# Later due times for queued splits in a two-block transformer kernel with float32 weights

## The chip, the core and the metric

The kernel runs on one core of one Trainium2 chip. The metric is the device time of one execution in microseconds (us). Five engines work side by side, each through its own queue in order: TensorE (PE, matrix products), VectorE (DVE), ScalarE (ACT), GpSimd (POOL) and SyncE (SP, which issues most transfers). Sixteen DMA engines move the data.

## The reference

The input `x` has 256 positions of 1024 channels. Two blocks follow one another, each of two layers. A layer is a feed-forward stage, a mixer and a second feed-forward stage, each added to `x`; the first block ends with a normalisation.

```python
x = x + 0.5 * swiglu(rms_norm(x, ffn1_norm[l]), ffn1_w_in[l], ffn1_w_out[l])   # 1024 -> 2 x 2816 -> 1024
x = x + mixer(rms_norm(x, mix_norm[l]), mix_w_in[l], ...)
x = x + 0.5 * swiglu(rms_norm(x, ffn2_norm[l]), ffn2_w_in[l], ffn2_w_out[l])
```

The mixer of the first block projects to q, k, v (8 heads of 64), to a Fourier branch and to two gates. Its attention adds a table of relative positions and a mask of columns to the scores. The mixer of the second block has three other kinds of attention; the change doesn't touch it. All weights are float32 and stay in the chip's main memory until they are used once.

## The kernel before, in words

**Products.** Every projection goes through `dense`. It takes weights in units of four 128-row tiles (1 MB, one transfer into one of four `raw` buffers, line 118) and splits each pair of tiles into a high and a low part, `whi` (a cast on ACT, line 341) and `wlo` (a subtraction on DVE, line 342). The activations are split in the same way (`xhi`, `xlo`, `hhi`, `hlo`). A product is then three matrix products (lines 145 to 147), so a pair of weight tiles feeds 2 tiles x 2 halves of the positions x 3 = 12 of them. `whi` and `wlo` have two buffers each, and two more while a feed-forward stage or the first mixer runs.

**Feed-forward stage (`ffn`).** Six steps compute gate and up product, 512 columns each (the last 256), with `h` = silu(gate) x up. `h` has to be transposed for the second product. Steps are grouped (`GROUPS`): steps 0 and 1 make eight 128-column tiles, steps 2 and 3 eight, step 4 four, step 5 two. For each group `queue_t` queues the transpose: `turned` transposes 32x32 blocks on DVE (`hB`, line 94), and two transfers issued by POOL carry it out to main memory and back in another order (`hop`, then `hT`, lines 96 and 97). Then `hT` is split into `hhi` and `hlo`, in pieces of up to four tiles and one half of the positions: four splits for a group of eight, two for the smaller ones. The second product is over all 22 tiles, once for each half `n` of the columns; it was written as 16 tiles, a `drain`, and 6 tiles. After `n` = 0, `queue_x` queues the same kind of transpose for the first half of the new `x`, with four parts.

**The queue.** `later(fn, ticks)` puts a function into a list with a due time; `advance` raises the tick by one and runs the first function that is due, one a tick; `drain` runs all that is left. `unit` calls `advance` after each split of a pair of weight tiles, so a tick is one such split:

```python
ins = self.split(hi[:, :m, :off], lo[:, :m, :off], raw[:, j : j + m, :off])
with self.tc.issue_after(ins.ins):
    if not self.hold:
        self.advance()
```

`split` returns its subtraction. `issue_after` orders what is written inside the block behind that instruction, if it is on the same engine. Apart from such constraints the source's order isn't the order of an engine's queue: the framework's scheduler works through the program with times of its own, and an instruction enters its engine's queue when, by these times, its inputs are there and its buffer is free.

**First mixer (`mixer1`).** Four steps of 512 columns (q, k, v, Fourier). q and k are transposed by `turned` into `qT` and `kT`, and split into `qh`, `kq`, `kzh` after all four steps, when the queue has been drained. `bias1` loads the table of a pair of heads by four transfers of 96 KB (`rawb`, line 437, issued by ACT) into one of the four `raw` buffers, and adds the column mask on DVE (`bias`, line 439, three buffers). Pairs 0 and 1 are loaded ahead of the first step, pairs 2 and 3 in the attention's loop. After the attention and the Fourier branch come four steps for the gates and the output products.

Of the kernel before, what the change touches and what calls it, by code (L numbers as in the profile page):

```python
# [18 lines left out]
P = 128  # L19
T = 2  # L20
# [6 lines left out]
class Net:  # L27
# [47 lines left out]

    def queue_t(self, h, nk, hhi, hlo, k0):
        hv = self.turned(lambda t: h[t], nk, self.b("hT", n=2048))
        lag = 7 if nk > 2 else 6
        step = min(nk, 4)
        for i in range(0, nk, step):  # L80
            for t in range(T):
                o = lambda d: d[:, k0 + i : k0 + i + step, t * P : (t + 1) * P].rearrange(
                    "p k (q j) -> p k q j", j=32)
                self.later(lambda hi=o(hhi), lo=o(hlo), s=hv[:, i : i + step, t]: self.split(hi, lo, s), lag)
# [116 lines left out]
    def queue_x(self, li):  # L201
        hv = self.turned(lambda t: self.x[:, t, :512], 4, self.xtile())

        def part(k):
            g = self.gcol[:, li, k : k + 1] if isinstance(li, int) else li[:, k : k + 1]
            for t in range(T):
                o = lambda d: d[:, k, t * P : (t + 1) * P].rearrange("p (q j) -> p q j", j=32)
                self.split(o(self.xhi), o(self.xlo), hv[:, k, t], scale=g)

        for k in range(4):  # L210
            self.later(lambda k=k: part(k), 7)

    def xt_half(self, n, li):
        nc = self.nc
# [29 lines left out]
    def ffn(self, w_in, w_out, nxt):  # L244
        nc = self.nc
        rs = None
        self.open()
        self.xtile = lambda: self.b("hT", n=2048)
        self.more(2)
        hhi = self.big.tile([P, 22, T * P], F32R, name=self.nm("hhi"), tag="hhi")  # L250
        hlo = self.big.tile([P, 22, T * P], F32R, name=self.nm("hlo"), tag="hlo")
        self.hold = True
        for c in range(6):
            if c < 5:
                pg = self.dense(self.xhi, self.xlo, KD, [(w_in, c * 512, 512)])
                pu = self.dense(self.xhi, self.xlo, KD, [(w_in, DFF + c * 512, 512)])
                w = 512
                gs, us = pg, pu
            else:
                pp = self.dense(self.xhi, self.xlo, KD, [(w_in, 2560, 256), (w_in, DFF + 2560, 256)])  # L260
                w = 256
                gs, us = pp, [q[:, 256:512] for q in pp]
            if rs is None:
                rs = self.rstd()
            if c == 0:
                self.hold = False
                self.drain()
            if c in GROUPS:
                h, c0 = [self.b("h", n=1024, bufs=4) for _ in range(T)], c
            for t in range(T):  # L270
                sl = self.b("sl", bufs=3)
                nc.scalar.activation(sl[:, :w], gs[t][:, :w], AF.Silu, scale=rs[:, t : t + 1])  # L272
                o = (c - c0) * 512
                nc.vector.scalar_tensor_tensor(h[t][:, o : o + w], us[t][:, :w], rs[:, t : t + 1], sl[:, :w],  # L274
                                               op0=ALU.mult, op1=ALU.mult)
            if c == 5 or c + 1 in GROUPS:
                self.queue_t(h, (o + w) // P, hhi, hlo, c0 * 4)
        for n in range(2):
            ps = self.dense(hhi, hlo, 16, [(w_out, n * 512, 512)], last=False)
            self.drain()  # L280
            self.dense(hhi, hlo, 6, [(w_out, n * 512, 512)], ps=ps, k0=16, first=False)
            for t in range(T):
                xs = self.x[:, t, n * 512 : (n + 1) * 512]
                nc.vector.scalar_tensor_tensor(xs, ps[t], 0.5, xs, op0=ALU.mult, op1=ALU.add)
            self.after(n, nxt)
        self.xtile = None
        self.more(0)
        self.close()
# [120 lines left out]
class Mix1:  # L409
# [18 lines left out]
    def bias1(self, l, p):  # L428
        nc = self.nc
        rp = self.a["rpbp"]  # L430
        bt = self.raw.tile([P, 4, 512], F32, name=self.nm("rawb"), tag="raw").rearrange("p a b -> p (a b)")[:, :768]
        bv = bt.rearrange("p (h e k) -> p h e k", h=2, e=6)
        for half in range(2):
            for h in range(2):
                src = bass.AP(tensor=rp.tensor, offset=((l * 8 + 2 * p + h) * 15 + 5 - half) * 127,
                              ap=[[1, 64], [127, 6], [1, 64]])
                nc.scalar.dma_start(out=bv[half * 64 : half * 64 + 64, h], in_=src)
        bias = self.big.tile([P, 768], F32, name=self.nm("bias"), tag="bias", bufs=3)
        nc.vector.tensor_tensor(bias.rearrange("p (h k) -> p h k", k=64)[:, :, ::-1],
                                bt.rearrange("p (h k) -> p h k", k=64),  # L440
                                self.cmask.unsqueeze(1).broadcast_to([P, 12, 64]), op=ALU.add)
        return bias

    def mixer1(self, l, nxt):
        nc, a, tc = self.nc, self.a, self.tc
# [6 lines left out]
        kzh = big.tile([P, 4, 2, 256], F32R, name=self.nm("kzh"), tag="mlo")  # L452
        kq = big.tile([P, 4096], F32R, name=self.nm("kq"), tag="m1th")
        kzl = kq[:, :2048].rearrange("p (k i t) -> p k i t", k=4, i=2)
        ql = kq[:, 2048:3072].rearrange("p (k t) -> p k t", k=4)
        qT = big.tile([P, 1024], F32, name=self.nm("qT"), tag="m1fhi")
        kT = big.tile([P, 1024], F32, name=self.nm("kT"), tag="m1flo")
        qh, vn = tl("qh", [P, 4, 256], F32R), tl("vn", [P, T, 512])
        u = big.tile([P, KD, 256], F32R, name=self.nm("u"), tag="mhi").rearrange("p (h t a) b -> p h t (a b)", h=2, t=2)
        uhi, ulo = u[:, 0], u[:, 1]  # L460
        bt = [self.bias1(l, p) for p in range(2)]
        self.zpad(kzh.bitcast(F32))
        self.zpad(kzl.bitcast(F32))
        rs = rq = None
        for c in range(4):
            ps = self.dense(self.xhi, self.xlo, KD, [(w_in, c * 512, 512)])
            if c == 0:
                rs = self.rstd()
                rq = self.sm.tile([P, T], F32, name=self.nm("rq"), tag="rq")
                nc.vector.tensor_single_scalar(rq, rs, 0.125, op=ALU.mult)  # L470
            if c < 2:
                h = []
                for t in range(T):
                    ht = self.b("h", bufs=4)
                    sc = (rq if c == 0 else rs)[:, t : t + 1]
                    if t == 0:
                        nc.scalar.activation(ht, ps[t], AF.Copy, scale=sc)
                    else:
                        nc.vector.tensor_scalar(out=ht, in0=ps[t], scalar1=sc, scalar2=None, op0=ALU.mult)
                    h.append(ht)  # L480
                turned = self.turned(lambda t, h=h: h[t], 4, qT if c == 0 else kT)
                qv, kv = (turned, None) if c == 0 else (qv, turned)
            elif c == 2:
                for t in range(T):
                    sc = rs[:, t : t + 1]
                    if t == 0:
                        nc.scalar.activation(vn[:, t], ps[t], AF.Copy, scale=sc)
                    else:
                        nc.vector.tensor_scalar(out=vn[:, t], in0=ps[t], scalar1=sc, scalar2=None, op0=ALU.mult)
            else:  # L490
                for t in range(T):
                    sc = rs[:, t : t + 1]
                    nc.scalar.activation(uhi[:, t], ps[t], AF.Copy, scale=sc)
                    nc.vector.scalar_tensor_tensor(ulo[:, t], ps[t], sc, uhi[:, t].bitcast(F32),
                                                   op0=ALU.mult, op1=ALU.subtract)
        self.drain()
        for t in range(T):
            o = lambda d: d[:, :, t * P : (t + 1) * P].rearrange("p k (q j) -> p k q j", j=32)
            self.split(o(qh), o(ql), qv[:, :, t])
            for i in range(2):  # L500
                r = slice(64 * i, 64 * i + 64)
                self.split(o(kzh[:, :, i])[r], o(kzl[:, :, i])[r], kv[r, :, t])
        ohi, olo = tl("ohi", [P, 4, 256], F32R), tl("olo", [P, 4, 256], F32R)
        for p in range(4):
            if p % 2 == 0:
# [8 lines left out]
                nc.vector.tensor_tensor(ona[:, t, (p % 2) * P : (p % 2 + 1) * P].rearrange("p (j d) -> p j d", j=2),  # L514
                                        po, rc.unsqueeze(2).broadcast_to([P, 2, 64]), op=ALU.mult)
            if p < 2:
                bt.append(self.bias1(l, p + 2))
            if p % 2 == 1:
                self.tr4(lambda j, t: ona[:, t, j * P : (j + 1) * P],
                         ohi[:, p - 1 : p + 1, :].rearrange("p a b -> p (a b)"),  # L520
# [22 lines left out]
        for c in range(4):  # L543
            ps = self.dense(self.xhi, self.xlo, KD, [(w_in, 2048 + c * 512, 512)])
# [3 lines left out]
            for t in range(T):  # L548
                d = th[:, t, c * 512 : (c + 1) * 512]
# [618 lines left out]
```

## Time and profile before

| | |
|---|---|
| time before, median of 3 runs | 2280.21 us (2274.0 to 2283.1) |
| profiled execution, its own time | 2291.64 us |
| its span, first to last instruction | 2289.8 us |
| PE busy | 99% of the span, 10446 products |
| PE weight loads (PEld) busy | 81% |
| DVE, ACT, POOL busy | 68%, 50%, 3% |
| DMA engines | 203 GB/s on average |
| mean granted clock of PE | 0.996 |

Engines' times overlap, so the shares don't add up. A product counts as busy until its result is written while the next one has begun, so a busy PE isn't one at its peak; but where PE is idle, it has nothing to do. The granted clock is a share of 2.4 GHz; it has two levels, and a mean between them over a stretch says how long each lasted.

### The profile page before, as it was taken

How to read it: one execution, taken by the hardware profiler on the slowest of the kernel's cores; microseconds unless marked ns; L12 is line 12 of the kernel's file. 1: busy time of each engine (PE TensorE's matmuls, PEld its weight loads, DVE VectorE, ACT ScalarE, POOL GpSimd, SP SyncE). 2: the span in 40 equal slices, each digit the busy share in tenths (PEclk: the TensorE clock that was granted, in tenths of full speed). 3: DMA queues.
4: the chain of work that ended last, by engine and by line, in shares of the span. 5: the costliest groups of instructions: out<-in, count | busy, mean ns of one | idle time of the engine just before them, and what ended most of it. 6: DMA issues, size and time to landing. Idle time of an engine off the chain costs nothing.

```text
span 2289.8 us, 27621 instructions
## 1 busy us (share of the span) xinstructions
PE 2260.2 (99%) x10446; PEld 1861.1 (81%) x10446; DVE 1547.2 (68%) x2549; ACT 1148.8 (50%) x1674; POOL 78.3 (3%) x133
## 2 busy tenths in 40 slices
PE   9999999999999999999999999999999999999999
PEld 7877888888788888887888887787887888778787
DVE  5666766666576776666666896765656668877564
ACT  5445545445444555445544555544444455455443
POOL 0001000000000000000000000000000000000000
PEclk9999999999999999999999999999999999999999
DMA  7767555776676745676766533467666755325673
GB/s 263 250 230 231 176 167 181 250 246 204 210 258 208 233 160 180 229 259 209 238 233 214 181 117 129 137 211 241 230 202 224 254 185 174 119 89 198 214 254 130
DMA packets 241669, 464.68 MB, mean 203 GB/s; under 512 B 22176, under 2 KB 47392, under 8 KB 239488
## 3 DMA queue, kind: packets, MB, share of 16 engines
q1 hardware_dynamic: 212272, 397.44, 52.6%
q0 software_dynamic: 14320, 60.69, 7.4%
q10 hardware_dynamic: 14944, 4.79, 1.1%
q8 instruction: 82, 1.34, 0.2%
q14 instruction: 51, 0.42, 0.1%
HBM read 433.00 MB, written 29.88 MB: 202 GB/s over the span
## 4 chain that ended last, share of the span: by engine, by line
PE 85%; issue 7%; DMA 5%; ACT 2%; DVE 1%; ACTq 0%; DVEq 0%; POOLq 0%
PE ps L146 26%; PE ps L145 26%; PE ps L147 26%; DMA hT<-hop 2%; PE ps L403 2%; DMA hop<-hB 2%; PE ps L396 1%; PE ps L891 1%; ACT whi L341 1%; DVE wlo L342 1%; PE ps L683 1%; PE ps L220 1%; PE ps L836 0%; PE ps L240 0%; ACT hhi L341 0%
## 5 line engine op out<-in xcount | busy, mean ns | idle before, releaser
L342 DVE TENSOR_TENSOR wlo<-raw,whi 128x1024 fp32r<-128x1024 f32 (+2 forms) x754 | 906.4, 1210 | 540.0 <-ACT whi L341 522.2
L341 ACT CAST whi<-raw 128x1024 fp32r<-128x1024 f32 (+2 forms) x754 | 777.9, 1044 | 780.9 <-PE ps L147 730.5
L146 PE MATMUL ps<-wlo,xhi 128*128 128x512 f32 (+2 forms) x2048 | 800.3, 392 | 8.3 <-DVE wlo L342 8.2
L145 PE MATMUL ps<-whi,xhi 128*128 128x512 f32 (+2 forms) x2048 | 786.2, 393 | 8.8 <-ACT whi L341 8.4
L147 PE MATMUL ps<-whi,xlo 128*128 128x512 f32 (+2 forms) x2048 | 789.6, 390 | 0.0
L146 PEld LDWEIGHTS ps<-wlo,xhi 128*128 128x128 f32 x2048 | 386.4, 189 | 90.8 <-DVE wlo L342 12.4
L145 PEld LDWEIGHTS ps<-whi,xhi 128*128 128x128 f32 x2048 | 385.3, 189 | 90.2 <-ACT whi L341 11.3
L147 PEld LDWEIGHTS ps<-whi,xlo 128*128 128x128 f32 x2048 | 386.6, 189 | 77.8 <-issue 0.5
L146 PE MATMUL ps<-wlo,hhi 128*128 128x512 f32 x704 | 273.9, 389 | 0.0
L147 PE MATMUL ps<-whi,hlo 128*128 128x512 f32 x704 | 273.9, 389 | 0.0
L145 PE MATMUL ps<-whi,hhi 128*128 128x512 f32 x704 | 271.3, 389 | 0.0
L145 PEld LDWEIGHTS ps<-whi,hhi 128*128 128x128 f32 x704 | 132.1, 188 | 27.6
L146 PEld LDWEIGHTS ps<-wlo,hhi 128*128 128x128 f32 x704 | 132.1, 188 | 27.4
L147 PEld LDWEIGHTS ps<-whi,hlo 128*128 128x128 f32 x704 | 132.1, 188 | 27.3
L94 DVE STREAM_TRANSPOSE hB<-h 128x1024 f32<-128x1024 f32 (+2 forms) x72 | 98.8, 1385 | 5.7 <-DMA hop<-hB 5.4
L342 DVE TENSOR_TENSOR hlo<-hT,hhi 128x512 fp32r<-128x512 f32 (+1 forms) x96 | 58.4, 643 | 56.5 <-ACT hhi L341 56.2
L341 ACT CAST hhi<-hT 128x512 fp32r<-128x512 f32 (+1 forms) x96 | 49.8, 582 | 87.8 <-DMA hT<-hop 87.8
L272 ACT ACTIVATE sl<-ps,rstd 128x512 f32<-128x512 f32 (+1 forms) x96 | 62.3, 651 | 50.9 <-PE ps L147 46.8
L96 POOL DMA_DIRECT2D hop<-hB x43 | 23.6, 548 | 1756.9 <-ACT whi L341 862.3
L391 ACT ACTIVATE pr<-ms,nmx 128x256 f32<-128x256 f32 (+1 forms) x112 | 51.3, 460 | 43.5 <-DVE nmx L386 38.7
L274 DVE SCALAR_TENSOR_TENSOR h<-ps,rstd,sl 128x512 f32<-128x512 f32 (+1 forms) x96 | 65.1, 697 | 2.9 <-PE ps L147 1.8
L97 POOL DMA_DIRECT2D hT<-hop x39 | 29.6, 758 | 184.6 <-DMA hop<-hB 103.6
(352 smaller groups left out, 1707.1 us busy)
## 6 DMA issues: line engine op xcount, KB each, us to landing
raw<-in_ffn_w_gu_dram SPq DMA_DIRECT2D x80, 1024.0 KB, 5.2
raw<-in_ffn_w_in_dram SPq DMA_DIRECT2D x79, 1024.0 KB, 5.2
raw<-in_ffn_w_out_dram SPq DMA_DIRECT2D x40, 1024.0 KB, 5.3
raw<-in_ffn_w_down_dram SPq DMA_DIRECT2D x40, 1024.0 KB, 5.1
raw<-in_mix_w_in_dram SPq DMA_DIRECT2D x32, 1024.0 KB, 6.5
raw<-in_w_gate_dram SPq DMA_DIRECT2D x24, 1024.0 KB, 5.2
hop<-hB POOLq DMA_DIRECT2D x16, 1024.0 KB, 5.9
hT<-hop POOLq DMA_DIRECT2D x16, 1024.0 KB, 6.2
```

Of the source, the lines that this page charges most:

```text
L94: nc.vector.transpose(ov[:, :, :, t, :], src(t)[:, : nk * P].rearrange("p (k i c) -> p k c i", c=4, i=32))
L96: nc.gpsimd.dma_start(out=hop.rearrange("q (i c) n -> (q i) (c n)", c=4), in_=hb)
L97: nc.gpsimd.dma_start(out=tile[:, :n].rearrange("p (q n) -> p q n", q=4), in_=hop.rearrange("q p n -> p q n"))
L145: mm(ps[:, :n], lhsT=lh, rhs=hi, start=start, stop=False)
L146: mm(ps[:, :n], lhsT=lh, rhs=lo, start=False, stop=False)
L147: mm(ps[:, :n], lhsT=ll, rhs=hi, start=False, stop=stop)
L272: nc.scalar.activation(sl[:, :w], gs[t][:, :w], AF.Silu, scale=rs[:, t : t + 1])
L274: nc.vector.scalar_tensor_tensor(h[t][:, o : o + w], us[t][:, :w], rs[:, t : t + 1], sl[:, :w], op0=ALU.mult, op1=ALU.mult)
L341: self.nc.scalar.copy(hi, src)
L342: return self.nc.vector.tensor_sub(lo, src, hi.bitcast(F32))
L391: nc.scalar.activation(pr[:, s], src[:, s], AF.Exp, bias=nm[:, j : j + 1], accum_out=den[:, j : j + 1])
L403: nc.tensor.matmul(po[:, j * 64 : (j + 1) * 64], lhsT=pt[:, q], rhs=v(j, st), start=(st == 0), stop=(st == ns - 1))
```

## The change

Due times are later: 11, 9 and 8 ticks for groups of eight, four and two tiles (7, 7 and 6 before), and 8 for the parts of `x` (7 before). The second product is one `dense` over 22 tiles, without the `drain`. In the first mixer `bias1` only loads, on SP's queue in place of ACT's, and a new `mask1` adds the mask. Pairs 0 and 1 are loaded after the first step, with their masks queued 7 ticks later; the splits of q are queued with 9 ticks and those of k with 7. Pair 2 is loaded after the four steps, pair 3 in the loop.

```diff
     def queue_t(self, h, nk, hhi, hlo, k0):
         hv = self.turned(lambda t: h[t], nk, self.b("hT", n=2048))
-        lag = 7 if nk > 2 else 6
+        lag = {8: 11, 4: 9, 2: 8}[nk]
...
         for k in range(4):
-            self.later(lambda k=k: part(k), 7)
+            self.later(lambda k=k: part(k), 8)
...
         for n in range(2):
-            ps = self.dense(hhi, hlo, 16, [(w_out, n * 512, 512)], last=False)
-            self.drain()
-            self.dense(hhi, hlo, 6, [(w_out, n * 512, 512)], ps=ps, k0=16, first=False)
+            ps = self.dense(hhi, hlo, 22, [(w_out, n * 512, 512)])
...
-                nc.scalar.dma_start(out=bv[half * 64 : half * 64 + 64, h], in_=src)
+                nc.sync.dma_start(out=bv[half * 64 : half * 64 + 64, h], in_=src)
+        return bt
+
+    def mask1(self, bt):
+        nc = self.nc
         bias = self.big.tile([P, 768], F32, name=self.nm("bias"), tag="bias", bufs=3)
...
-        bt = [self.bias1(l, p) for p in range(2)]
+        bt = []
...
+        part = lambda d, t: d[:, :, t * P : (t + 1) * P].rearrange("p k (q j) -> p k q j", j=32)
+        split_q = lambda t: self.split(part(qh, t), part(ql, t), qv[:, :, t])
+
+        def split_k(t):
+            for i in range(2):
+                r = slice(64 * i, 64 * i + 64)
+                self.split(part(kzh[:, :, i], t)[r], part(kzl[:, :, i], t)[r], kv[r, :, t])
...
-                qv, kv = (turned, None) if c == 0 else (qv, turned)
+                if c == 0:
+                    qv = turned
+                    rb = [self.bias1(l, p) for p in range(2)]
+                    for r in rb:
+                        self.later(lambda r=r: bt.append(self.mask1(r)), 7)
+                    for t in range(T):
+                        self.later(lambda t=t: split_q(t), 9)
+                else:
+                    kv = turned
+                    for t in range(T):
+                        self.later(lambda t=t: split_k(t), 7)
...
         self.drain()
-        for t in range(T):
-            o = lambda d: d[:, :, t * P : (t + 1) * P].rearrange("p k (q j) -> p k q j", j=32)
-            self.split(o(qh), o(ql), qv[:, :, t])
-            for i in range(2):
-                r = slice(64 * i, 64 * i + 64)
-                self.split(o(kzh[:, :, i])[r], o(kzl[:, :, i])[r], kv[r, :, t])
+        rb = self.bias1(l, 2)
...
             if p < 2:
-                bt.append(self.bias1(l, p + 2))
+                bt.append(self.mask1(rb))
+                if p == 0:
+                    rb = self.bias1(l, 3)
```

## Rows read from the trace of the kernel before

**Rows 1.** The page, parts 1 and 5: engines; one group (busy, mean | idle before).
```profile
PE 2260.2 (99%) x10446; PEld 1861.1 (81%) x10446; DVE 1547.2 (68%) x2549; ACT 1148.8 (50%) x1674; POOL 78.3 (3%) x133
...
L341 ACT CAST hhi<-hT 128x512 fp32r<-128x512 f32 (+1 forms) x96 | 49.8, 582 | 87.8 <-DMA hT<-hop 87.8
```

**Rows 2.** Waits of PE: what for, us in total, times, longest.
```profile
PE ps L145 <- ACT whi L341: 8.9, 9, 2.1
PE ps L146 <- DVE wlo L342: 8.2, 9, 2.8
```

**Rows 3.** Stretches: length, busy us (count) of PE, PEld, DVE, ACT, POOL, clock, DMA.
```profile
118.00:126.00 8.00, 5.89 (x25) 4.35 (x24) 5.05 (x7) 5.03 (x7) 0.00 (x0) 1.00 0.16 40
224.00:236.00 12.00, 9.24 (x34) 7.10 (x33) 6.16 (x6) 4.46 (x5) 0.76 (x1) 0.86 0.97 265
601.00:615.00 14.00, 11.60 (x37) 8.73 (x36) 8.00 (x10) 6.10 (x9) 0.00 (x0) 0.76 0.43 143
728.00:734.00 6.00, 4.88 (x21) 3.47 (x20) 4.68 (x7) 3.46 (x7) 0.00 (x0) 1.00 1.04 396
1555.00:1561.00 6.00, 4.30 (x18) 3.01 (x17) 3.73 (x6) 5.00 (x7) 0.00 (x0) 1.00 0.04 14
1738.00:1748.00 10.00, 7.79 (x27) 5.78 (x26) 7.30 (x9) 5.02 (x7) 0.00 (x0) 0.83 0.35 106
2166.00:2173.00 7.00, 4.16 (x18) 2.87 (x17) 4.25 (x6) 5.03 (x7) 0.00 (x0) 1.00 0.05 16
...
400.00:500.00 100.00, 100.00 (x443) 82.81 (x442) 67.66 (x67) 48.41 (x57) 5.21 (x8) 1.00 0.73 246
414.00:426.00 12.00, 12.00 (x55) 9.94 (x54) 6.76 (x9) 6.09 (x8) 0.37 (x1) 1.00 0.64 222
```

**Rows 4.** Timeline of ACT, 114 to 128 us: start, us, instruction, [idle before, releaser].
```profile
114.75 1.05 ACT L341 CAST whi<-raw 128x1024 fp32r<-128x1024 f32 x1 [3.80 <-PE ps L147]
119.68 2.18 ACT L341 CAST hhi<-hT 128x512 fp32r<-128x512 f32 x4 [3.87 <-DMA hT<-hop]
121.77 2.94 ACT L341 CAST whi<-raw 128x1024 fp32r<-128x1024 f32 x3
```

**Rows 5.** Timeline of DVE, 120 to 125 us.
```profile
120.33 1.89 DVE L342 TENSOR_TENSOR hlo<-hT,hhi 128x512 fp32r<-128x512 f32 x3 [3.27 <-ACT hhi L341]
122.84 1.23 DVE L342 TENSOR_TENSOR wlo<-raw,whi 128x1024 fp32r<-128x1024 f32 x1 [0.61 <-ACT whi L341]
123.98 0.68 DVE L342 TENSOR_TENSOR hlo<-hT,hhi 128x512 fp32r<-128x512 f32 x1
```

**Rows 6.** Timeline of ACT in the next feed-forward stage, 417 to 424 us.
```profile
419.62 2.18 ACT L341 CAST hhi<-hT 128x512 fp32r<-128x512 f32 x4 [1.00 <-DMA hT<-hop]
421.71 2.94 ACT L341 CAST whi<-raw 128x1024 fp32r<-128x1024 f32 x3
```

**Rows 7.** Timeline of DVE in the first mixer, layer 0, 218 to 232 us.
```profile
227.97 0.96 DVE L439 TENSOR_TENSOR bias<-rawb,cmask 128x768 f32<-128x768 f32 x1 [4.68 <-DMA rawb<-in_rpbp_dram]
228.85 3.49 DVE L342 TENSOR_TENSOR wlo<-raw,whi 128x1024 fp32r<-128x1024 f32 x3
```

**Rows 8.** The tile rawb: ns of an issue (min/median/max); us to landing.
```profile
L437 ACTq DMA_DIRECT2D rawb<-in_rpbp_dram x32: 602/637/1225, 172.8 to 754.4; - x32
...
DMA to landing us min/median/max: 2.7/4.2/11.4
```

**Rows 9.** Timeline of DVE, start of the first mixer in layer 1.
```profile
724.26 1.81 DVE L439 TENSOR_TENSOR bias<-rawb,cmask 128x768 f32<-128x768 f32 x2
```

**Rows 10.** Timeline of ACT, the same place.
```profile
730.51 1.99 ACT L341 CAST whi<-raw 128x1024 fp32r<-128x1024 f32 x2 [2.81 <-DMA raw<-in_mix_w_in_dram]
```

**Rows 11.** DMA, 195 to 250 us: a queue (packets, MB, share); an issue (median to landing).
```profile
q10 hardware_dynamic: 3200, 0.79, 9.6%
...
raw<-in_mix_w_in_dram SPq DMA_DIRECT2D x11, 1024.0 KB, 7.2
```

## The prediction, made before the result was known

> **What bounds the kernel.** The first view to read is the page. Its part 1 shows the tensor engine (PE) busy for 2260.2 of the 2289.8 us of the span [rows 1]; only 29.6 us are idle, so work taken off the vector engine (DVE) or the scalar engine (ACT) is worth nothing by itself. The work on PE is the same before and after the change. What the change can give back is idle PE and what idle PE does to its clock. The second view is the waits of PE: 8.9 us for `whi` (the cast on ACT) and 8.2 us for `wlo` (the subtraction on DVE), in nine waits each [rows 2]; in the page's group of these casts ACT itself waits 87.8 us for `hT`, 32 times [rows 1]. So the splits of the weights come late in a few places. The third view, the table of stretches, gives these places and the price of each [rows 3]: length less PE busy is the idle time, and (1 - granted clock) x length is the time lost at the lower clock (1.2 instead of 2.4 GHz).
>
> - Feed-forward stages, five places: 118 to 126 us 2.1 idle; 601 to 615 2.4 idle and 3.4 by the clock (0.76); 1555 to 1561 1.7; 1738 to 1748 2.2 and 1.7 by the clock (0.83); 2166 to 2173 2.8. Sum 11.2 + 5.1 = 16.3 us.
> - First mixer, layer 0: 224 to 236 us 2.8 idle and 1.7 by the clock (0.86), 4.5 us. Layer 1: 728 to 734 us 1.1 us. Sum 5.6 us.
>
> In a stretch without such a place PE is never idle (400 to 500 us, 443 products in 100 us, so 0.226 us a product). A tick of the queue is one split of a weight tile, which feeds 12 products: 2.7 us.
>
> **Part 1: the longer lags in the feed-forward stages.** Why is the weight split late there? The timelines of ACT and DVE around 118 us show it. ACT casts `whi` at 114.75, then waits 3.87 us until the transposed `hT` has landed, casts `hhi` four times in a row (2.18 us), and only at 121.77 casts the next `whi` [rows 4]. DVE does three `hlo`, then `wlo` at 122.84, then the fourth `hlo` [rows 5]. The lag of 7 queues the four splits at ticks 7, 8, 9 and 10, the first behind the weight split of tick 7. If both halves of a split were held back by its tick, no four casts could stand in a row. They do, in all 16 groups of this size, of which two are shown [rows 4, 6]. The code says why: `unit` runs the queued split inside `issue_after(ins.ins)`, `ins` is the subtraction, and the constraint holds only for instructions on that engine, DVE. The fourth `hlo` does stand behind the `wlo` of its tick at 122.84 [rows 5], while the fourth `hhi` stands ahead of that tick's `whi` [rows 4]. So the lag holds `hlo`, and `hhi` goes where the scheduler believes `hT` to have landed, between the `whi` of ticks 9 and 10.
>
> A lag of 11 changes nothing in that: the transposes and both transfers are queued where they were, so ACT is to stand before the same `hhi`, for the same transfer, ahead of the same `whi`. `wlo` at 122.84 follows that cast; the three `hlo` are over by then (120.33 + 1.89) and delay nothing. What the change removes is the fourth `hlo` (0.68 us) and its like between later subtractions, where PE isn't waiting. Its value here is bounded by 0 and 16.3 us; I take 0, by these rows [rows 4, 5].
>
> Does the delay cost anything? Counted from the end of the fourth gate-and-up step, splits of the second group of eight run at ticks 11 to 14 (before 7 to 10), the transposes of the group of four at 9 and 10, those of the last two tiles at 15 and 16, the splits of these at 17, 18 and 20, 21. The second product's eleven weight pieces are ticks 13 to 23; it reads the group of four at tick 21 and the last two tiles at 23. The tightest cover is two ticks, 5.4 us, and weights are split ahead of their products besides. Cost 0; if the cover went, one DVE split (0.68 us) would stand in front of PE in each of eight stages, 5 us. `drain` in the middle of the second product finds nothing left at `n` = 0 and two parts of `x` at `n` = 1; these now go at ticks 10 and 11 of eleven, ahead of the next stage's first weight split. One `dense` over 22 tiles emits the same pieces as 16 and then 6. Cost 0.
>
> **Part 2: masks of the first mixer.** In layer 0 DVE waits 4.68 us for the table `rawb` of head pair 2, adds the mask at 227.97, and three `wlo` follow from 228.85 [rows 7]; PE waits for the first. That mask was put early into DVE's queue and its table took up to 11.4 us from issue to landing [rows 8]. After the change the tables of pairs 0 and 1 come after the first projection step, their masks stand behind the `wlo` of ticks 7 and 8, and the table of pair 2 is asked for after all four steps. At 227 no mask then stands ahead of a `wlo`. The splits of q move behind ticks 9 and 10 on DVE only; ACT still casts them when it thinks `qT` there. Gain 4.5 us.
>
> In layer 1 the two masks (724.26, 1.81 us) held two of the four `raw` buffers at the start of the stage [rows 9], and the next weights, loaded into these, came so late that ACT waited 2.81 us and cast at 730.51 [rows 10]. After the change the weights of the first step get these buffers first. Gain 1.1 us.
>
> What is added: the mask of pair 2 still has no tick, so DVE can stand before it again, a few us later. From below nothing: the same mask of layer 1 shows no such place [rows 3]. From above what layer 0 paid, 4.5 us for each layer. I take 0: the request moves away from the projections' transfers, and one of two layers already shows it free. The issues of the tables leave ACT (32 x 0.637 us, 20.4 us [rows 8]) and go to SP's queue; ACT is off the path but for the waits named, so 0. Behind them on SP stand weight loads: that is a rival below.
>
> **Sum.** 16.3 x 0 - 4.5 - 1.1 + 0 = -5.6 us. The profiled execution took 1.8 us more than its span, 2291.6 us, and would become 2286.0. The median of the runs shown is 11.4 us under it; I take the same difference from the median: 2280.2 - 5.6 = 2274.6 us.
>
> **Rivals.**
>
> A. The lag does move ACT's casts. Then the five feed-forward places go as well: 2274.6 - 16.3 = 2258.3. For it: in the next stage `hhi` waits only 1.00 us [rows 6] and PE is not idle (414 to 426) [rows 3], so a little less waiting is enough, and four ticks are 10.9 us. Against it: the timelines [rows 4, 5], where DVE obeys the tick and ACT doesn't. Chance 0.25.
>
> B. Slower: the two tables now hold two of four `raw` buffers from the first step until ticks 7 and 8, so the weights of the second and third step go through the other two. A buffer then has two ticks, 5.4 us, for a load, and loads there take 7.2 us [rows 11], 1.8 late. A cast 7.0 us after the one before it [rows 4] cost PE 2.1 us, so I estimate that some 4.9 us of lateness are free; two loads in a row decide it when each takes over 5.4 + 2.45 = 7.9 us. At 11.4, the slowest landing of that stretch [rows 8], they would be 12.0 late, 7.1 of it on PE, in two layers 14.2: 2274.6 + 14.2 = 2288.8. Against it: the median is below the point. Chance 0.12.
>
> The mask tables went by a queue of their own, 3200 packets at 9.6% of 16 engines over 55 us, 26 ns each [rows 11]; a table has 1600, 2.6 us of all engines. The Trainium skill ("DMA: Bandwidth & Descriptors", section "Two DMAs through the same engine are not ordered") says that within one queue of one DMA engine descriptors start in order. By that rule a weight load on SP's queue would stand behind a table, 9.8 us instead of 7.2: 3.9 us on PE a layer, 2274.6 + 7.8 = 2282.4; no row here shows it, since tables and weights were on different queues. It stands within B.
>
> C. The mask of pair 2 waits in its new place as it did in layer 0, and nothing is won: 2280. Chance 0.11.
>
> **Numbers.** The forecast has 0.52, A 0.25, B 0.12, C 0.11. What a measurement can tell from no change is 0.5%, 11.4 us: faster means under 2268.8, slower over 2291.6. Faster: A and a little of the forecast, 0.28. Slower: the upper part of B, 0.07. Same 0.65. The forecast's own range is 2269 to 2281; the range reaches down to the middle of A and up to B: 2258 to 2288.
>
> **What would show it.** Right: in every group of eight, ACT's four `hhi` still stand in a row between the same two `whi` with a wait for `hT`, while `hlo` alternates with `wlo`; PE's idle places in the feed-forward stages remain, and those at 224 and 728 are gone. Wrong: `hhi` behind the `whi` of ticks 11 to 14 and no wait for `hT` (A); ACT waiting for `raw` in the second and third projection step (B); DVE idle before a mask, with PE idle after it (C).

## The result, and the profile after

| | before | after |
|---|---|---|
| time, median of 6 runs each | 2280.41 us (2274.0 to 2283.1) | 2294.02 us (2289.34 to 2299.77) |
| ratio to before, 95% interval | | 1.0064 [1.0046, 1.0082] |

The changed kernel is 0.6% slower, 13.6 us; forecast were 5.6 us less. The page of the changed kernel, parts 1 and 5 (columns as in [rows 1]; ACT's cast stands on line 339 now, DVE's subtraction on 340):

```profile
PE 2262.5 (99%) x10446; PEld 1861.2 (81%) x10446; DVE 1539.4 (67%) x2549; ACT 1148.9 (50%) x1674; POOL 78.3 (3%) x133
...
L339 ACT CAST hhi<-hT 128x512 fp32r<-128x512 f32 (+1 forms) x96 | 49.8, 582 | 94.9 <-DMA hT<-hop 94.9
```

The work is the same. ACT waits for `hT` even a little longer than in [rows 1] (94.9 against 87.8 us). The waits of PE in the changed kernel:

```profile
PE ps L145 <- ACT whi L339: 9.4, 8, 4.0
PE ps L146 <- DVE wlo L340: 5.1, 9, 0.8
...
PE ps L145 <- ACT oTc L241: 2.1, 1, 2.1
```

The sum for `whi` is about that of [rows 2], but its longest wait is twice as long, and the last line is new: `oTc` is a cast in the second mixer, which the change doesn't touch.

For a fair comparison the kernel before was profiled again (first experiment below): that execution has a span of 2276.3 us, the one of [rows 3] 2289.8, and the timed runs agree with the shorter. Here are the two mixers of each block as whole stages, from one residual sum to the next (columns as in [rows 3]); first the kernel before in its second profile, in order first mixer layer 0 and 1, second mixer layer 0 and 1:

```profile
192.09:350.56 158.47, 157.61 (x785) 132.36 (x784) 116.35 (x204) 82.69 (x134) 8.53 (x12) 1.00 0.62 199
715.88:875.85 159.97, 158.04 (x785) 132.16 (x784) 117.18 (x206) 83.33 (x136) 8.97 (x13) 1.00 0.61 200
1239.80:1482.50 242.70, 241.89 (x1236) 196.27 (x1235) 195.69 (x548) 135.43 (x256) 4.38 (x11) 1.00 0.45 143
1846.10:2088.79 242.69, 241.88 (x1236) 196.26 (x1235) 195.66 (x548) 135.42 (x256) 4.38 (x11) 1.00 0.45 144
```

And the changed kernel:

```profile
191.45:351.42 159.97, 158.71 (x785) 132.19 (x784) 116.25 (x205) 82.95 (x135) 8.54 (x12) 1.00 0.61 194
719.02:884.85 165.83, 160.63 (x785) 134.28 (x784) 117.55 (x205) 83.69 (x135) 9.03 (x13) 0.98 0.60 194
1248.30:1491.00 242.70, 241.89 (x1236) 196.25 (x1235) 195.68 (x549) 135.46 (x256) 4.39 (x11) 1.00 0.45 143
1855.37:2103.28 247.91, 244.98 (x1236) 198.67 (x1235) 196.87 (x548) 135.14 (x256) 4.38 (x11) 0.99 0.45 141
```

The lengths differ by 1.5, 5.9, 0 and 5.2 us, 12.6 of the 15.0 us between the two spans; the rest is spread over the eight feed-forward stages. So the loss has two large places: the first mixer of layer 1, which the change rewrote, and the second mixer of layer 1, which it didn't.

**First mixer, layer 1.** The chain of waits of the changed kernel, 745 to 760 us (start, us, what):

```profile
744.31 0.88 DVE bias L441
...
745.21 12.79 DMA raw<-in_mix_w_in_dram
...
758.10 1.05 ACT whi L339
```

A mask gives its `raw` buffer back at 745.19 (744.31 + 0.88); only then can SP issue the weight load that wants it, which takes 12.79 us. The cast stands behind it, and PE, which gets its first product from it at 759.2 us. SP's own timeline (start, us, count) shows when the tables and the weights were issued:

```profile
708.24 5.32 SPq L435 DMA_DIRECT2D rawb<-in_rpbp_dram  x8
721.25 24.33 SPq L118 DMA_DIRECT2D raw<-in_mix_w_in_dram  x6
747.00 11.61 SPq L435 DMA_DIRECT2D rawb<-in_rpbp_dram  x8
```

Two tables are issued at 708, some 36 us before their masks run. Until 745 their two buffers are away from the weights; five of the six loads of 1 MB issued from 721 on go through the other two, and the sixth is the one behind the mask. It is the last piece of the fourth projection step.

That load was slow as well as late: the median load of the stage takes 5.9 us (shown below). While it was under way, from 745 to 758 us, the DMA engines were busy nearly all the time (302 GB/s). In the same stretch they carried the tables of pairs 2 and 3 (1997 of the 3175 packets have less than 512 bytes), a transpose and a bias of the gates. Which of these slowed the load was not tried separately. An estimate from these rows: PE ran dry 4.0 us before 759.2, so at 755.2; a load asked for at 745.2 and followed by a cast of 1.05 us would have come in time if it had landed within some 8.9 us. The late request and the slow landing make the wait together.

The changed kernel's two places of [rows 3] that were to be mended, and the stretch around the new gap on PE:

```profile
222.00:236.00 14.00, 13.56 (x60) 10.86 (x59) 9.52 (x11) 7.16 (x9) 0.76 (x1) 1.00 1.15 284
...
724.00:734.00 10.00, 10.00 (x46) 8.29 (x45) 7.31 (x18) 6.13 (x10) 0.00 (x0) 1.00 0.70 243
752.00:768.00 16.00, 11.97 (x40) 9.31 (x40) 6.81 (x8) 4.36 (x5) 0.76 (x1) 0.79 1.00 290
```

At 752 PE is idle for 4.0 us and loses 3.4 us (0.21 x 16) by the lower clock. The idle places at 224 and 728 are indeed gone, all but 0.4 us.

**Feed-forward stages.** ACT in the changed kernel, 114 to 122 us, the place of [rows 4]:

```profile
115.26 1.05 ACT L339 CAST whi<-raw 128x1024 fp32r<-128x1024 f32 x1 [3.80 <-PE ps L147]
117.38 2.18 ACT L339 CAST hhi<-hT 128x512 fp32r<-128x512 f32 x4 [1.06 <-DMA hT<-hop]
119.47 2.94 ACT L339 CAST whi<-raw 128x1024 fp32r<-128x1024 f32 x3
```

Four `hhi` in a row between the same two `whi`, waiting for the same transfer; so it is in all 16 groups of eight. On DVE, 123 to 127 us, `hlo` now stands singly between `wlo` (compare [rows 5]):

```profile
123.48 0.69 DVE L340 TENSOR_TENSOR hlo<-hT,hhi 128x512 fp32r<-128x512 f32 x1
...
125.78 1.17 DVE L340 TENSOR_TENSOR wlo<-raw,whi 128x1024 fp32r<-128x1024 f32 x1
126.89 0.67 DVE L340 TENSOR_TENSOR hlo<-hT,hhi 128x512 fp32r<-128x512 f32 x1
```

PE is idle in such places as before (near 419, 601, 1740 and 2171 us); how many and how long differs from execution to execution.

### The profile page after: what moved, and what is told of

The parts are those of the page before. It is cut to its first block, busy times and chain, and to the rows that moved or that the text cites. A ratio compares the mean times of both kernels' runs of the same rounds, so it can differ in the third digit from the quotient of the medians.

```text
span 2291.3 us, 27586 instructions
## 1 busy us (share of the span) xinstructions
PE 2262.5 (99%) x10446; PEld 1861.2 (81%) x10446; DVE 1539.4 (67%) x2549; ACT 1148.9 (50%) x1674; POOL 78.3 (3%) x133
## 4 chain that ended last, share of the span: by engine, by line
PE 83%; issue 7%; DMA 6%; ACT 2%; DVE 2%; SPq 0%; ACTq 0%; DVEq 0%; POOLq 0%
PE ps L146 25%; PE ps L145 25%; PE ps L147 25%; DMA hT<-hop 2%; PE ps L401 2%; DMA hop<-hB 2%; DMA raw<-in_mix_w_in_dram 2%; ACT whi L339 1%; DVE wlo L340 1%; PE ps L394 1%; PE ps L908 1%; PE ps L700 1%; PE ps L220 1%; PE ps L853 0%; PE ps L240 0%
## 5 line engine op out<-in xcount | busy, mean ns | idle before, releaser
L339 ACT CAST hhi<-hT 128x512 fp32r<-128x512 f32 (+1 forms) x96 | 49.8, 582 | 94.9 <-DMA hT<-hop 94.9
```

The lines of the kernel that those rows point to most:

```text
L339: self.nc.scalar.copy(hi, src)
```

## The experiments

Ratios are to the kernel before, run beside each, with 95% intervals. Stage lengths are of one profiled execution.

### The kernel before again

No edit.

> The kernel before, unchanged: a second trace of it. Theory: the profiled execution of before (span 2289.8 us) was about 11 us above its timed runs because the transposed tiles landed late in five feed-forward stages; a trace of an execution near 2280 us then shows fewer or shorter waits of PE for the weight casts there, 10 to 12 us less in sum over the feed-forward stages. Rival: the waits are the same in every execution, and the profile itself costs the 11 us, evenly; then the new trace shows the same five places within 2 us in sum. Ratio to before 1.000 either way.

Measured 2279.42 us, ratio 1.0005 [0.9992, 1.0018]. The rival falls: the execution profiled here took 2278.1 us, near the median. The theory had the place of the difference only in part. Of the 13.5 us between the two spans 7.4 lie in the feed-forward stages, where 10 to 12 were expected, 4.7 in the first mixer of layer 0 (163.19 against 158.47 us) and 1.3 in the second mixer of layer 0 (244.00 against 242.70). The first mixer of layer 1 takes 160.0 us in one and 160.1 in the other. This execution's place around 224 us (columns as in [rows 3]), and the mask of pair 2 on DVE:

```profile
218.00:236.00 18.00, 18.00 (x81) 14.92 (x80) 12.03 (x14) 10.23 (x13) 1.67 (x3) 1.00 1.07 319
```

```profile
222.78 0.96 DVE L439 TENSOR_TENSOR bias<-rawb,cmask 128x768 f32<-128x768 f32 x1 [1.76 <-DMA rawb<-in_rpbp_dram]
```

In this execution the mask waited 1.76 us instead of 4.68 [rows 7] and PE is not idle at all. The 4.5 us that the forecast credited were in one of the two executions, so they aren't a cost that the kernel always has.

### The two parts alone

The feed-forward part: the lags, 8 ticks for the parts of `x`, one `dense` over 22 tiles.

```diff
-        lag = 7 if nk > 2 else 6
+        lag = {8: 11, 4: 9, 2: 8}[nk]
```

> Only the feed-forward part of the change (lags of 11, 9 and 8 ticks, 8 for the parts of x, one product over 22 tiles); the first mixer as before. Theory (ACT's casts of hT are not held by the ticks): same as before within 4 us, and ACT still casts hhi four times in a row between the weight casts of ticks 9 and 10. Rival: the shifted subtractions or another order in later stages cost the time; then 2284 to 2294 us.

Measured 2284.11 us, ratio 1.0016 [1.0003, 1.0029]: no gain, and perhaps a loss of some 3.7 us that no stage shows clearly. The time lies where the theory's range ends and the rival's begins, so it doesn't decide between them; the order of ACT's casts is as the theory says, four `hhi` in a row in all 16 groups of eight. The mixer part alone:

```diff
+                    rb = [self.bias1(l, p) for p in range(2)]
+                    for r in rb:
+                        self.later(lambda r=r: bt.append(self.mask1(r)), 7)
```

> Only the first mixer's part of the change; the feed-forward stages as before. Theory: this part brings the slowdown, because the mask tables now stand on SP's queue ahead of weight loads; 2288 to 2294 us, with one weight load of 10 us or more in layer 1 and PE waiting for a weight cast behind it. Rival: it is neutral, 2276 to 2284 us, and the time comes from the feed-forward part.

Measured 2290.98 us, ratio 1.0051 [1.0033, 1.0069]: first mixer layer 1 165.1 us, second mixer layer 1 247.4. This part is nearly all of the loss. The time is the one that the theory gave; its cause, SP's queue, is tried next.

### Which resource: queue or buffers

The whole change, tables issued by ACT again:

```diff
-                nc.sync.dma_start(out=bv[half * 64 : half * 64 + 64, h], in_=src)
+                nc.scalar.dma_start(out=bv[half * 64 : half * 64 + 64, h], in_=src)
```

> The changed kernel with the mask tables issued by ACT again, as before the change, and all else changed. Theory (weight loads behind tables on one queue): the long weight load of layer 1 falls from 12.8 to under 9 us and the wait of PE behind it (4.2 us and the lower clock after it, 7 us together) goes; 2284 to 2288 us. Rival (the two tables hold two of four weight buffers, whatever the queue): no change, 2290 to 2297 us.

Measured 2295.38 us, ratio 1.0058 [1.0042, 1.0075], as the rival had it. The first mixer of layer 1 takes 163.3 us (165.8 in the changed kernel), that of layer 0 162.4 (160.0): in sum the same, 325.7 and 325.8 us. Its slowest weight load in layer 1 still takes 10.6 us. Taking the tables off SP's queue gives nothing back on the whole. Then the whole change, with the first two tables in memory that is idle at that time:

```diff
-        bt = self.raw.tile([P, 4, 512], F32, name=self.nm("rawb"), tag="raw")...
+        if p < 2:
+            bt = self.big.tile([P, 1024], F32, name=self.nm("rawb"), tag=("m1ohi", "m1olo")[p])[:, :768]
```

> The changed kernel, with the mask tables of head pairs 0 and 1 in memory that is not yet used at that time (that of ohi and olo) instead of two of the four weight buffers; they are still issued on SP after the first projection step, and the tables of pairs 2 and 3 stay where they were. Theory (the tables hold two of four weight buffers, so the weights of the second and third projection step are asked for late): the first mixer of layer 1 goes back from 165.8 us to about 160, layer 0 from 160 to 158.5, and the time from 2294 to about 2287, or 2283 if the order at the end of the second mixer of layer 1 is undisturbed as well. Rival (the tables' many small packets on SP's queue delay the weight loads, whoever holds the buffers): layer 1 stays at 163 to 166 us and the time at 2291 to 2296.

> As the run before it, and the tables issued by ACT instead of SP. Theory of the held buffers: no difference to the run before it beyond 2 us (2283 to 2288), first mixer of layer 1 about 160 us. Rival of the queue: this one, and not the run before it, goes back to about 160 us and 2283 to 2288.

Issued by SP: 2294.93 us, ratio 1.0063 [1.0051, 1.0075]. By ACT: 2287.65 us, ratio 1.0035 [1.0022, 1.0048]. The first mixer of layer 1 takes 160.2 us in the one and 159.8 in the other: at this stage the buffers are the cause, the queue is not. On the total both expectations failed: the first run is no faster than the change, and the second is 7.3 us faster than the first, where the theory allowed 2; by the time alone the rival of the queue would have been right. From the first run, the first mixer of layer 1, the second mixer of both layers and a place in the feed-forward stage between:

```profile
718.47:878.67 160.20, 158.51 (x785) 132.06 (x784) 117.84 (x205) 83.77 (x135) 9.01 (x13) 1.00 0.61 192
1246.52:1494.17 247.65, 243.93 (x1236) 197.55 (x1235) 196.45 (x548) 135.09 (x256) 4.38 (x11) 0.99 0.44 141
1858.46:2103.78 245.32, 242.77 (x1236) 196.21 (x1235) 195.94 (x549) 135.00 (x256) 4.38 (x11) 1.00 0.45 142
...
984.00:1000.00 16.00, 13.22 (x51) 10.25 (x50) 9.46 (x11) 7.09 (x10) 0.00 (x0) 0.89 0.44 152
```

The two first mixers give back 7.0 us against the trace of the changed kernel (layer 0 takes 158.57). The second mixer, now late in both layers (247.65 and 245.32 against 242.7), takes 2.4 us more in sum than there, and the feed-forward stages 6.5 more; the last row shows one stall of these (2.8 us idle and 1.8 us by the clock). With the tables issued by ACT the second mixer has 242.70 and 242.68 us, 7.6 us less in sum, about the difference of the two medians. (The two profiled executions differ by 3.9 us only; that of the second run took 3.5 us more than its median.) So the issuing engine does matter, but downstream, in a stage that holds no table.

### Holding the cast

The mixer of the kernel before, the lags of the change, and the queued work held behind both halves of the tick's split:

```diff
-            with self.tc.issue_after(ins.ins):
+            with self.tc.issue_after(ins.ins), self.tc.issue_after(self.cast.ins):
```

(`split` keeps its cast in `self.cast`.)

> The mixer of the kernel before, the feed-forward lags of the change, and the queued work held behind ACT's cast of the tick as well as behind DVE's subtraction. Theory (the lags bring nothing because ACT's casts are not held): the four casts hhi no longer stand in a row between two whi, PE's waits for whi and wlo in the feed-forward stages go (in the run with the lags alone 1.55 + 1.0, 2.0 + 1.0, 1.7 + 1.0 us idle and 3.4 us by the clock, 11.7 us), and 2284 becomes 2270 to 2275. Rival (the transposed hT lands late whatever the order, or holding both halves makes another cast late): 2280 to 2288, with PE's waits for whi still 5 us or more.

Measured 2267.82 us, ratio 0.9946 [0.9934, 0.9958], faster than both kernels. ACT at the place of [rows 4]:

```profile
119.77 0.62 ACT L339 CAST hhi<-hT 128x512 fp32r<-128x512 f32 x1 [0.82 <-DMA hT<-hop]
120.61 1.06 ACT L339 CAST whi<-raw 128x1024 fp32r<-128x1024 f32 x1 [0.22 <-PE ps L147]
121.57 0.61 ACT L339 CAST hhi<-hT 128x512 fp32r<-128x512 f32 x1
126.05 1.06 ACT L339 CAST whi<-raw 128x1024 fp32r<-128x1024 f32 x1 [3.87 <-PE ps L147]
```

Casts of `hhi` and `whi` alternate, and ACT waits for PE rather than for `hT`. The group of the page in this run, then the waits of PE, first in the run with the lags alone, then in this one:

```profile
L339 ACT CAST hhi<-hT 128x512 fp32r<-128x512 f32 (+1 forms) x96 | 55.6, 579 | 22.3 <-DMA hT<-hop 22.3
```

```profile
PE ps L145 <- ACT whi L339: 6.2, 7, 1.9
PE ps L146 <- DVE wlo L340: 4.2, 7, 0.8
```

```profile
PE ps L146 <- DVE wlo L340: 2.2, 3, 1.1
...
PE ps L145 <- ACT whi L339: 1.4, 4, 0.6
```

The run with the lags alone differs by the hold only. Against it ACT's wait for `hT` falls from 94.5 to 22.3 us and PE's waits for `whi` and `wlo` together from 10.4 to 3.6; the mean granted clock goes from 0.999 to 1.000. The mechanism of the theory holds; the time is 2.2 us under its range. Now the same hold with the old lags:

> The kernel before with its old lags, and ACT's casts held by the tick. Theory (lag and hold are both needed): held at tick 7, ACT stands before hhi even earlier than it does now, since the transposed hT has not landed by then, and the weight casts behind it come later: slower than before, 2285 to 2330. Rival (the hold alone is what brings the gain): 2268 to 2274.

Measured 2276.75 us, ratio 0.9978 [0.9969, 0.9988]: the expectation fails, and so does its rival. The weight casts don't come later than before. The group in this run:

```profile
L341 ACT CAST hhi<-hT 128x512 fp32r<-128x512 f32 (+1 forms) x96 | 52.0, 581 | 81.4 <-DMA hT<-hop 81.4
```

The hold only says what an instruction may not precede; the scheduler still puts three of the four casts where it believes `hT` to land, ahead of the `whi` of tick 10, and the hold moves only the fourth. The hold is worth 4.7 us against the kernel before; hold and lag together 12.5. Where the 4.7 us are won isn't shown: PE's waits for `whi` and `wlo` are 10.0 us in this trace and 9.7 in the second trace of the kernel before.

### Queued splits of q and k alone

The kernel before, with the splits of q (9 ticks) and k (7) queued, tables and masks as they were.

> The kernel before, with the splits of q and k queued as in the change and nothing else of it: the tables are issued by ACT ahead of the first projection step, their masks are added there. Theory (the loss in the first mixer is the tables' alone): first mixer of layer 1 at 159.5 to 160.5 us, time 2277 to 2282. Rival (the queued splits of q and k, or the other order of instructions that they give, cost the time): layer 1 at 162 us or more, time 2285 to 2292.

Measured 2279.94 us, ratio 0.9998 [0.9986, 1.001]; first mixer layer 1 160.1 us. The queued splits are free within the noise (0.1%), and the first mixer's loss is the tables'.

### The change with the cast held

The edit of the hold, on the whole change; then the same with the tables of pairs 0 and 1 in memory of their own.

> The whole change, and ACT's casts held by the tick as in the run before (lags and hold with the old mixer: 2267.8 us). Theory (two independent costs): the feed-forward waits go as there, the first mixer still pays for the tables in the weight buffers, 5 us in layer 1 and 1 to 1.5 in layer 0, so 2273 to 2276; the first mixer of layer 1 at 164 to 166 us. The second mixer of layer 1 has the order of the kernel before in this program (oTc cast right behind the first weight cast) and is to take 242.7 us, not 247.9. Rival (the second mixer's 5 us come from the queued masks and splits themselves): 247 us there and 2278 to 2281.

> As the run before it, and the tables of pairs 0 and 1 in memory of their own. Theory: what is left of the loss goes, first mixer of layer 1 at 160 us, time 2267 to 2270, no better than the lags and the hold with the old mixer (2267.8), because the mixer part itself gains nothing in a typical execution. Rival (the mixer part does gain its 5.6 us once its tables hold no weight buffer): 2262 to 2264.

Measured 2275.86 us, ratio 0.998 [0.997, 0.9989], and 2271.16 us, ratio 0.9956 [0.9943, 0.997]. The first mixer of layer 1 takes 164.99 us in the first and 158.45 in the second: nothing but the tables' place differs, so two held buffers cost 6.5 us there, by these two traces (the medians of the whole differ by 4.7 us). The tile `raw` in the first mixer of layer 1, first in the changed kernel, then in the second of these runs:

```profile
  DMA raw<-in_mix_w_in_dram: 13.4, 4
...
DMA to landing us min/median/max: 5.1/5.9/12.8
```

```profile
  PE ps L147: 23.1, 13
  ACT whi L339: 12.2, 10
...
DMA to landing us min/median/max: 5.2/6.1/8.0
```

The first lines are what engines waited for before instructions on this tile (us, times). With four buffers nobody waits for a weight load, though the median load is no faster. The first of these runs, which has the hold as well but lends two buffers, waits like the changed kernel (12.5 us, 4 times, its slowest load 13.0 us). The first expectation was wrong about the second mixer: that program has the late `oTc` too, and 247.3 us there, as its rival said; its time agrees with the theory all the same. For the second run the time is just above the theory's range. The rival (5.6 us of gain once the buffers are free) isn't settled by the time, since this run's second mixers take 246.10 and 245.29 us, 6.0 more than those of the kernel before. Its first mixers settle it: 158.57 and 158.45 us against 158.47 and 159.97 are a gain of 1.4 us.

### The second mixer

Behind which instruction does the cast of `oTc` stand? ACT in the changed kernel, second mixer of layer 1:

```profile
2053.53 1.05 ACT L339 CAST whi<-raw 128x1024 fp32r<-128x1024 f32 x1 [1.60 <-PE ps L147]
...
2058.34 1.05 ACT L339 CAST whi<-raw 128x1024 fp32r<-128x1024 f32 x1 [2.72 <-PE ps L147]
...
2060.35 1.03 ACT L339 CAST whi<-raw 128x1024 fp32r<-128x1024 f32 x1
2061.28 0.58 ACT L241 ACTIVATE oTc<-ps 128x512 fp32r<-128x512 f32 x1
```

The same in the second profile of the kernel before:

```profile
2043.79 1.05 ACT L341 CAST whi<-raw 128x1024 fp32r<-128x1024 f32 x1 [3.54 <-PE ps L147]
...
2046.55 0.60 ACT L241 ACTIVATE oTc<-ps 128x512 fp32r<-128x512 f32 x1 [0.66 <-PE ps L240]
```

The instructions are the same; in the changed kernel three weight casts stand ahead of `oTc`, before it was one. The edit holds the weight casts of the second half behind it:

```diff
+                if n == 1 and i < 2:
+                    with self.tc.issue_after(last.ins):
+                        y = self.dense(hi, lo, kk, segs)
```

> The whole change, and in the second mixer the weight casts of the second half are held behind the cast of oTc on ACT, which is the order that the kernel before has there. Theory (the loss of 5 us in the second mixer of layer 1 is that order alone): the stage goes from 247.9 to 243 to 244 us and the time from 2294 to 2289 or 2290. Rival (the stage is slow for another reason, its first part being late): 247 us and 2293 to 2296.

Measured 2291.9 us, ratio 1.0047 [1.0035, 1.006], the stage 245.9 us: half of what the theory asked for, and a time between its range and the rival's. Two stretches of the changed kernel, then of this one:

```profile
2034.00:2044.00 10.00, 9.46 (x49) 6.92 (x48) 8.96 (x44) 5.20 (x19) 0.00 (x0) 0.83 0.17 52
2058.00:2068.00 10.00, 7.88 (x29) 6.01 (x28) 6.03 (x9) 4.85 (x7) 0.00 (x0) 0.83 0.56 197
```

```profile
2036.00:2046.00 10.00, 9.46 (x48) 6.99 (x48) 8.95 (x44) 4.97 (x18) 0.00 (x0) 0.83 0.16 52
2060.00:2070.00 10.00, 8.69 (x38) 6.40 (x37) 7.47 (x11) 7.83 (x10) 0.00 (x0) 1.00 0.44 155
```

And the first of them in the second profile of the kernel before:

```profile
2024.00:2034.00 10.00, 9.46 (x56) 6.70 (x56) 8.94 (x45) 5.93 (x19) 0.00 (x0) 1.00 0.16 54
```

At `oTc` PE's idle time falls from 2.12 to 1.31 us and the clock doesn't drop; that part is the order. The drop some 20 us earlier (0.83, 1.7 us) stays, with the same 0.54 us of idle PE that the kernel before has there at clock 1.00; the run with queued splits of q and k, which has the old order, shows it as well (0.83, and 243.96 us for the stage). So does the kernel before in its first trace, in the second mixer of layer 0: 0.54 us idle and clock 0.83 from 1424 to 1434 us. So it doesn't need the change, and its cause stays open. PE waits over 2 us for `oTc` in all five programs in which SP issues the tables and nothing holds the order (mixer part alone, change, own buffers, and the two with the hold), and in none of those in which ACT issues them. Why the scheduler's times move this cast so far downstream was not tried.

## Why the prediction was wrong, by its steps

**Part 1, the lags: right.** DVE obeys the tick, ACT doesn't, and the lags gain nothing [rows 4 to 6]. Holding the cast shows it: the ratio goes from 1.0016 with the lags alone to 0.9946, 0.7% or 16 us; against the kernel before it is 12.5 us. That the first figure meets the 16.3 us of [rows 3] at which rival A was priced is in part luck, since that price was read from the slow execution: in the second trace the feed-forward stages are 7.4 us shorter without any edit. Rival A needed one more edit. The cost of the longer delay, taken as 0, may be up to 0.29%; the interval of the lags alone just excludes none.

**Part 2, the gain of 5.6 us: wrong in size.** The places were named rightly and are gone. But their price was read from one execution whose own time, 2291.6 us, lay 11.4 us over the median, and the forecast carried the whole gain over to the median. In a second execution the same two places show 0 and 1.1 us of idle PE, of which the change can win no more than that. With tables in memory of their own and the cast held, the two stages take 1.4 us less than there.

**Part 2, the tables' cost of 0: the step that failed.** The sum has no term for the two tables in the weight buffers; moving them was taken as free. Rival B had the mechanism: two of four buffers held from the first step until the masks, loads late, ACT waiting for `raw`. It looked for the wait in the second and third step, after two slow loads in a row; in layer 1 it came in the fourth, after one. It had a chance of 0.12 because the median load of 7.2 us [rows 11] was under the deciding 7.9. Not the median decides, but the slowest of some ten loads: 12.8 us here, asked for late and carried beside the tables of pairs 2 and 3. The trace of before had a warning that the argument left out: in the first mixer of layer 0 one weight load took 9.2 us and the next 7.8. The 11.4 us that B put in their place is no weight load's; it is the landing of a table [rows 8]. B's price was 7.1 us a layer; measured are 5.9 in layer 1 and 1.5 in layer 0, so its nearness to the first is partly luck. The tables held their buffers longer than the ticks suggested, 36 us rather than seven ticks of 2.7, since they were issued at 708 us, before the first step's products had run, and SP's order is the scheduler's as well. The queue's order, which B's second paragraph adds, is not what happened: the slow load was issued ahead of the second pair of tables, and with tables on either queue the stage is equal (160.2 and 159.8 us). The Trainium skill ("DMA: Bandwidth & Descriptors", section "Issuing engines are not separate DMA queues") says that SP's and ACT's transfers share the same 16 engines; the equal stages agree with it.

**A term that was missing.** 5.2 us were lost in the second mixer of layer 1, of which no step spoke. The prediction itself says that an engine's order is worked out by a scheduler; it then treated every stage that the diff doesn't touch as unchanged. The late `oTc` explains 2.1 us idle and one drop of the clock (1.7 us), shown by the forced order in part; another drop of 1.7 us is not explained, and the kernel before has one like it in one of its traces, so this part may be chance.

Summed by stages of the two traces, 1.5 + 5.9 + 5.2 = 12.6 us and 2.4 us spread over the rest, where 5.6 us less were forecast. C said that nothing would be won, which came near, but by a wait of pair 2's mask that the changed kernel doesn't show; B was right on the cost.

## What to carry to other kernels

A due time holds only the instructions that are ordered behind something on their own engine: look at each engine's timeline to see which half of a queued step obeys it, and hold every half (here the lags alone won nothing, the hold alone 4.7 us, both 12.5). A buffer lent from a load ring for something slow costs what the slowest load then costs, so count how long it is held from issue to release, compare with the tail and not the median of the landings, and see what else the DMA engines carry at that time. Price a stall from more than one execution, and where a scheduler orders the program, compare the stages that the diff doesn't touch as well.

## What was not expected of the hardware

An issue for a table on SP took 624 ns in the median, but up to 4.27 us while a weight load and other transfers were under way (eight issues in 11.61 us at 747). In the run with the hold and tables of their own the longest was 0.99 us. In the second mixer of layer 1 the mean granted clock was 0.83 over 10 us in the changed kernel's trace, which is 3.4 us at 1.2 GHz, and 1.00 at the same place in the second trace of the kernel before, with the same 0.54 us of idle PE in both. No run shows why.
